# Two DRAM tensors for the experts' rows, and eight index buffers in place of five

## The chip, the cores and the metric

The kernel runs on one core of one Trainium2 chip. The metric is the device time of one execution in microseconds (us). The core has five engines that each run their own list of instructions: PE (matmul), DVE (vector), ACT (scalar), POOL (GpSimd) and SP, which here only issues DMAs. They meet by semaphores.

## The reference

512 tokens of width 1024 pass through two blocks. The first ends in a mixture of experts, and that is where the change lies. Cut to what matters:

```python
scores = sigmoid(h @ router_w)                        # 64 experts
idx = top_8(scores + router_b, in the best 4 of 8 groups of experts)
wts = scores[idx] / sum(scores[idx]) * 2.5
def body(acc, blk):                                   # blocks of up to 128 tokens of one expert
    tok, wt, e = blk
    xb = h[tok]
    hid = silu(xb @ w1[e]) * (xb @ w3[e])             # 1024 -> 256
    return acc.at[tok].add(wt[:, None] * (hid @ w2[e])), None   # 256 -> 1024
routed, _ = scan(body, zeros, blocks)
shared = (silu(h @ sw1) * (h @ sw3)) @ sw2
f = routed + shared
x = layernorm(DN_ALPHA * x + g2 * f, ln2_w, ln2_b)    # DN_ALPHA = 2 ** 0.25
```

The second block (attention and a feed-forward network) follows and is not touched.

## The kernel before, in words

**Lists.** The 64 experts are worked off as 39 token lists of at most 128 tokens: eleven with one expert each (the "singles", numbered 0 to 10), then thirteen of two experts that share one list (the "pairs"), two more singles and thirteen more pairs. The program calls a list b and an expert's job e0, e1, ... by its place in the sequence.

**One list.** `find(b)` makes the list: DVE compares each token's place with a row of numbers (`oh`, L1324), PE multiplies that with the token numbers (`sel`), and DVE writes `idx` (L1329, the token numbers as integers) and `wt` (L1330, the weights). POOL gathers the 128 rows from the DRAM tensor `hrows` by an indirect DMA (`xg`, L1683). PE transposes them (`tsp`, L1149); ACT and DVE split them in two parts, `xh` and `xl` (L122, L123), since each product is made of three matmuls of split factors (L128 to L130). 24 matmuls give `gu`; ACT applies silu, DVE multiplies (`hid`, L1344). PE transposes `hid` (`ht`), it is split (`th`, `tl`), and 12 matmuls give `y`. DVE multiplies `y` by the gate `g2b` into `yo` (L1443, two halves). POOL adds `yo` to the rows of the DRAM tensor `yrows` by an indirect DMA that accumulates (L1687, the scatter).

**Weights.** Each expert has three pieces (g0, g1, o2) of 128x2048 in 32 bits. SP loads them, ACT casts them to a high part (h), DVE subtracts that to get a low part (l, L123, 128x2048).

**What sets the order.** The loop over jobs at the end of `moe` writes the second half of a job (`down` and the scatter) behind the first half of the next one (`late`). `find` runs two lists ahead. The framework's scheduler orders each engine's list by its own estimates, and it puts a wait wherever a buffer is used again: a tile with `bufs=5` is written again five uses later, once its last reader is done. For `idx` the last reader is the scatter's DMA. DMAs on one DRAM tensor that write are ordered one behind the other.

**Beginning and end.** The four 128-token parts of the shared expert run first. POOL adds x (already times DN_ALPHA) to their rows (L1461), and SP writes them into `yrows` (L1462): the start value of the sum. `overflow` (L1629, a loop) would take lists beyond the 39; here it runs no iteration, but at its entry and exit the engines wait for all DMAs. Behind it `combine` loads x from `yrows` (L1607) and normalizes it: DVE's `l2st`, `l2mv`, POOL and DVE's `l2rs`, then x scaled by `ln_w`, `ln_b`.

Of the kernel before, what the change touches and what calls it, by code (L numbers as in the profile page):

```python
# [13 lines left out]
F32 = mybir.dt.float32  # L14
# [3 lines left out]
U32 = mybir.dt.uint32  # L18
AF = mybir.ActivationFunctionType
OP = mybir.AluOpType  # L20
# [4 lines left out]
P = 128  # L25
D = 1024
KT = D // P
T = 512
TC = 256
TA = T + TC  # L30
NT = T // P
# [62 lines left out]
class Kernel:  # L94
# [1273 lines left out]
    def moe(self):  # L1368
# [3 lines left out]
        nc, I = self.nc, self.I  # L1372
        V, G = nc.vector, nc.gpsimd
        E = 64
        self.hrows = self.dram.tile([T, D], F32, name="hrows")
        self.yrows = self.dram.tile([T, D], F32, name="yrows")

        cx = self.mcx = ExitStack()
        sp = self.pool("slots", ctx=cx, side="right")
# [12 lines left out]
        with ExitStack() as c2:  # L1392
            self.grans(self.pool("ew", ctx=c2), 2, 5)
            es = self.pool("es", bufs=2, ctx=c2)
# [4 lines left out]
            def job(name, gr, x, put, wt=None, first=True, last=True):  # L1399

                hid = self.hidden(name, gr, es, *x, wt)
                if late:
                    late.pop()()
                late.append(lambda: sums.append(self.down(name, gr[2], es, hid, put, () if first else sums[-1], first, last)))

            sums, idx, ahead = [], {}, []
# [11 lines left out]
            def find(b):  # L1418

                if b < len(groups):  # L1420
                    idx[b] = [es.tile([P, n], dt, tag=tag, name=f"{tag}{b}", bufs=5) for n, dt, tag in ((1, U32, "idx"), (2, F32, "wt"))]
                    self.select(es, idx[b][0], idx[b][1][:, :share(b)], *groups[b][0], f"sel{b}")

            def begin():
                find(0)
                self.gather(xg[0], idx[0][0])
                find(1)
# [7 lines left out]
            def putter(name, end):  # L1435

                yo = []

                def put(half, py):
                    if half == 0:  # L1440
                        yo.append(es.tile([P, D], F32, tag="yo", name="yo" + name))
                    hs = slice(half * 512, half * 512 + 512)
                    V.tensor_tensor(yo[0][:, hs], py, self.g2b[:, hs], OP.mult)  # L1443
                    if half == 1:
                        end(yo[0])
                return put

            src = lambda w: [w[:, i * 2048:(i + 1) * 2048] for i in range(3)]
            with ExitStack() as c3:
                sh = []  # L1450

                def shared_load(i):
                    sh.append(self.load(src(I["sh_pack"])[i], f"shg{i}"))

                def shared_parts(i):
                    sh[i] = self.parts(sh[i])

                def shared(t):

                    def end(y):  # L1460
                        G.tensor_tensor(y, y, self.x[:, t], OP.add)  # L1461
                        nc.sync.dma_start(self.yrows[t * P:(t + 1) * P, :], y)  # L1462
                    job(f"sh{t}", sh, self.hT[t], putter(f"sh{t}", end))
                shared = {"L": shared_load, "W": shared_parts, "s": shared, "e": first_load, "E": first_parts}
                self.mix_out(c3, shared, begin)
# [7 lines left out]
            gr = old = None  # L1473
            for n, (b, c, h) in enumerate(jobs):
                if n == 1:
                    with ExitStack() as c3:
                        self.order(self.pool("ol", ctx=c3))
                new = n == 0 or jobs[n - 1][1] != c
                if h == 0:
                    find(b + 2)  # L1480
                if new:
                    if c < NX:
                        w = I["exp_pack"][c]
                    else:
                        with self.tc.issue_after(self.loaded):
                            er = nc.values_load(self.ids[:, c - NX:c - NX + 1], engines=(mybir.EngineType.SP,), min_val=0, max_val=63)
                        w = I["exp_pack"][bass.ds(er, 1)].rearrange("e p n -> p (e n)")
                    w = src(w)

                    if c < 2:  # L1490
                        gr, ahead = ahead[:2], ahead[2:]
                        gr = [g if ("E", 2 * c + n) in MIX else self.parts(g) for n, g in enumerate(gr)]
                    else:
                        gr = [self.gran(w[i], f"e{c}g{i}") for i in range(2)]
                if old:
                    old[0].append(self.gran(old[1], f"e{c}o2"))
                old = (gr, w[2]) if new else None
                if h == 0:
                    x = xg[b % 2]
                    if b:  # L1500
                        self.gather(x, idx[b][0])
                    xh = ep.tile([P, KT, P], F32R, tag="xh", name=f"xh{b}")
                    xl = ep.tile([P, KT, P], F32R, tag="xl", name=f"xl{b}")
                    self.transpose_split(xh, xl, [x])
                job(f"e{n}", gr, (xh, xl), putter(f"{b}", lambda y, b=b: self.scatter(y, idx[b][0])),
                    idx[b][1][:, h:h + 1], h == 0, h == share(b) - 1)
                if not new:
                    late.pop()()
# [91 lines left out]
    def combine(self, loaded, done):  # L1600

        nc = self.nc
        V, G = nc.vector, nc.gpsimd
        with self.mcx as cx:
            m2 = self.pool("cmb", bufs=NT, ctx=cx, side="right")
            for t in range(NT):
                nc.sync.dma_start(self.x[:, t], self.yrows[t * P:(t + 1) * P, :])  # L1607
            loaded()
            lw, lb = self.ln2
            for t in range(NT):  # L1610
                x = self.x[:, t]
                if t < 2:
                    self.normalize(m2, x, x, lw, lb, "l2")
                else:
                    mu, rs = self.ln_stats(m2, x, LN_EPS, "l2")
                    V.scalar_tensor_tensor(x, x, mu, lw, OP.subtract, OP.mult)
                    nc.scalar.activation(x, x, AF.Copy, scale=rs)
                    G.tensor_tensor(x, x, lb, OP.add)
                done(t)

    def overflow(self, sp):

        nc, I = self.nc, self.I
        V, G = nc.vector, nc.gpsimd
# [3 lines left out]
        n = nc.values_load(self.ntot, min_val=0, max_val=E)  # L1628
        with self.tc.For_i(0, n):  # L1629
            with ExitStack() as cx:  # L1630
# [19 lines left out]
                gr = [self.gran(w[:, i * 2048:(i + 1) * 2048], f"ovg{i}") for i in range(3)]  # L1650
# [14 lines left out]
                idx = op.tile([P, 1], U32, name="oidx")  # L1665
                wt = op.tile([P, 1], F32, name="owt")
                self.select(op, idx, wt, lambda t: pj[:, t:t + 1], lambda t: tk[:, t:t + 1], "osel")
                x = op.tile([P, D], F32, name="oxg")
                G.memset(x, 0.0)
                self.gather(x, idx)  # L1670
                xh = op.tile([P, KT, P], F32R, name="oxh")
                xl = op.tile([P, KT, P], F32R, name="oxl")
                self.transpose_split(xh, xl, [x])
                yo = op.tile([P, D], F32, name="oyo")
# [2 lines left out]
                    hs = slice(half * 512, half * 512 + 512)  # L1677
                    V.tensor_tensor(yo[:, hs], py, self.g2b[:, hs], OP.mult)
                self.down("ov", gr[2], op, self.hidden("ov", gr, op, xh, xl, wt), put)
                self.scatter(yo, idx)  # L1680

    def gather(self, x, idx):
        self.nc.gpsimd.indirect_dma_start(out=x, out_offset=None, in_=self.hrows, in_offset=bass.IndirectOffsetOnAxis(ap=idx, axis=0),  # L1683
                                          bounds_check=T - 1, oob_is_err=False)

    def scatter(self, y, idx):
        self.nc.gpsimd.indirect_dma_start(out=self.yrows, out_offset=bass.IndirectOffsetOnAxis(ap=idx, axis=0), in_=y, in_offset=None,  # L1687
                                          bounds_check=T - 1, oob_is_err=False, compute_op=OP.add)


# [599 lines left out]
```

## Time and profile before

| | |
|---|---|
| median of 3 runs | 2989.39 us (2989.31 to 2990.99) |
| the profiled execution | 2991.12 us, its span 2989.3 us |
| PE busy | 2672.5 us, 89% of the span |
| DVE busy | 1880.2 us, 63% |
| ACT busy | 1263.1 us, 42% |
| POOL busy | 530.0 us, 18% |

The span is the part of the execution that the profiler sees. Busy shares are means over the whole program. The expert stage runs from about 740 to 1521 us; the singles fill its first third.

### The profile page before, as it was taken

What the parts mean: (1) busy time and instruction counts of PE and PEld (TensorE: products, weight loads), DVE (VectorE), ACT (ScalarE), POOL (GpSimd) and SP (SyncE); (2) the same over time, 40 slices, a digit from 0 to 9 for tenths busy, and PEclk for the clock granted to TensorE, in tenths of its full rate; (3) what the DMA queues carried; (4) which work ended last, traced back from release to release, by engine and by line L of the source; (5) the groups of instructions that cost most, each with busy time, mean ns of one, the idle gap of its engine ahead of it and who ended that gap; (6) DMA issues with size and microseconds to landing.
All of it is one profiled execution on the core that took longest, in us unless ns stands there. A gap on an engine that the chain in (4) does not pass through costs nothing. (4 is left out here: it accounts for less than half of the span.)

```text
span 2989.3 us, 46834 instructions
## 1 busy us (share of the span) xinstructions
PE 2672.5 (89%) x18599; PEld 2261.3 (76%) x18603; DVE 1880.2 (63%) x3463; ACT 1263.1 (42%) x1976; POOL 530.0 (18%) x514
## 2 busy tenths in 40 slices
PE   6999776779776999999959999999998999999998
PEld 4787565668655777777758999887877989987786
DVE  6974767768765899899958943332326974433233
ACT  4232432323343676676735554321225556422221
POOL 1001341121223213222233420000002341000000
PEclk9999777989887999999979999999999999999999
DMA  6541002124576999999932112222222211222222
GB/s 213 198 151 43 5 26 38 31 95 163 205 232 218 327 389 359 329 376 355 342 119 72 57 57 71 85 95 82 92 93 100 69 59 50 86 85 90 94 92 78
DMA packets 134348, 427.52 MB, mean 143 GB/s; under 512 B 51194, under 2 KB 77754, under 8 KB 95728
## 3 DMA queue, kind: packets, MB, share of 16 engines
q1 hardware_dynamic: 122896, 391.77, 36.7%
q0 software_dynamic: 11232, 32.74, 4.5%
q8 instruction: 147, 2.41, 0.3%
q14 instruction: 73, 0.60, 0.1%
HBM read 398.25 MB, written 34.37 MB: 145 GB/s over the span
## 5 line engine op out<-in xcount | busy, mean ns | idle before, releaser
L1687 POOL DMA_INDIRECT yrows<-yo,idx x39 | 109.6, 2810 | 321.3 <-DVE yo L1443 203.1
L2066 DVE TENSOR_TENSOR hd<-hd,ffu 128x512 f32<-128x512 f32 x44 | 30.3, 688 | 178.0 <-PE ffu L130 178.0
L1683 POOL DMA_INDIRECT xg<-hrows,idx x39 | 86.3, 2213 | 214.5 <-PE tsp L1149 135.0
L122 ACT CAST hh<-hd 128x512 fp32r<-128x512 f32 x44 | 27.2, 618 | 109.6 <-DVE hd L2066 109.6
L137 POOL TENSOR_TENSOR nm1s<-nm1s,cst 128x1 f32<-128x1 f32 x4 | 2.2, 550 | 381.6 <-DVE nm1s L136 373.7
L137 POOL TENSOR_TENSOR frss<-frss,cst 128x1 f32<-128x1 f32 x4 | 2.2, 548 | 372.2 <-DVE frss L136 372.2
L2085 DVE TENSOR_TENSOR x<-x,dn 128x512 f32<-128x512 f32 x32 | 22.0, 686 | 66.0 <-PE dn L130 66.0
L871 PE MATMUL qa<-PR,qk 64*64 64x128 f32 (+1 forms) x384 | 27.0, 362 | 33.1 <-DVE PR L977 12.7
L1329 DVE CAST idx<-sel 128x1 uint32<-128x1 f32 x39 | 6.0, 154 | 77.9 <-DMA yrows<-yo,idx 60.5
L1958 ACT COPY pTs<-pT 128x128 f32<-128x128 f32 (+3 forms) x96 | 39.9, 428 | 35.5 <-PE pT L1956 33.4
L2065 ACT ACTIVATE hd<-ffg 128x512 f32<-128x512 f32 x44 | 26.0, 592 | 67.2 <-PE ffg L130 67.0
L1925 DVE MAX8 m<-sc 128x8 f32<-128x256 f32 (+2 forms) x96 | 52.9, 555 | 1.0
L1926 DVE MATCH_REPLACE8 sc<-m,sc 128x256 f32<-128x256 f32 (+2 forms) x96 | 52.0, 542 | 0.0
L123 DVE TENSOR_TENSOR xl<-tsp,xh 128x512 fp32r<-128x512 f32 x78 | 51.0, 682 | 1.4 <-ACT xh L122 1.3
L1149 PE MATMUL tsp<-cst,xg 128*128 128x128 f32 x312 | 45.5, 283 | 6.8 <-DMA xg<-hrows,idx 6.8
L237 DVE SCALAR_TENSOR_TENSOR adas<-adar,cs,adas 128x256 f32<-128x256 f32 x112 | 49.9, 475 | 1.3
L122 ACT CAST xh<-tsp 128x512 fp32r<-128x512 f32 x78 | 42.8, 592 | 18.2 <-PE tsp L1149 18.2
L871 PEld LDWEIGHTS qa<-PR,qk 64*64 64x64 f32 x384 | 19.2, 193 | 37.2 <-issue 14.4
L1960 PE MATMUL po<-va,pTs 128*128 128x64 f32 x320 | 45.0, 275 | 1.0 <-ACT pTs L1958 0.3
L1960 PEld LDWEIGHTS po<-va,pTs 128*128 128x128 f32 x320 | 40.3, 191 | 6.0 <-ACT pTs L1958 5.2
L1149 PEld LDWEIGHTS tsp<-cst,xg 128*128 128x128 f32 x312 | 36.4, 145 | 9.9 <-issue 7.1
L1712 PE MATMUL nm0p<-nm0d,x 128*128 128x128 f32 x64 | 14.1, 414 | 30.3 <-DVE l2rs L136 21.7
(4409 smaller groups left out, 10492.3 us busy)
## 6 DMA issues: line engine op xcount, KB each, us to landing
adar<-in_ada_w_dram SPq DMA_DIRECT2D x16, 1024.0 KB
x<-in_w_in_pack_dram SPq DMA_DIRECT2D x11, 1024.0 KB
adaw<-in_ada_w_dram SPq DMA_DIRECT2D x8, 1024.0 KB
x<-in_x_dram SPq DMA_DIRECT2D x8, 512.0 KB
xs<-x SPq DMA_DIRECT2D x8, 512.0 KB
x<-xs SPq DMA_DIRECT2D x8, 512.0 KB
hrows<-h SPq DMA_DIRECT2D x4, 512.0 KB
yrows<-yosh SPq DMA_DIRECT2D x4, 512.0 KB
```

What stands on the lines that cost most here:

```text
L122: nc.scalar.copy(h, src)
L123: nc.vector.tensor_tensor(l, src, h.bitcast(F32), OP.subtract)
L237: V.scalar_tensor_tensor(acc, wt[:, k], c, acc, OP.mult, OP.add)
L871: nc.tensor.matmul(pq[h][cs, x, m, :nw], qk[hs, x, m, cs], PR[hs, m, :nw, cs], start=True, stop=True)
L1149: nc.tensor.transpose(pt[:, (k - k0) * w + j * P:(k - k0) * w + (j + 1) * P], x[:, k * P:(k + 1) * P], self.ident)
L1683: self.nc.gpsimd.indirect_dma_start(out=x, out_offset=None, in_=self.hrows, in_offset=bass.IndirectOffsetOnAxis(ap=idx, axis=0), bounds_ch ...
L1687: self.nc.gpsimd.indirect_dma_start(out=self.yrows, out_offset=bass.IndirectOffsetOnAxis(ap=idx, axis=0), in_=y, in_offset=None, bounds_ch ...
L1925: V.max(m8, s)
L1926: V.match_replace(s, m8, s, PICKED)
L1958: nc.scalar.copy(st, pt)
L1960: nc.tensor.matmul(out, st[:, s], v[:, s, c0:c0 + w], start=(s == 0), stop=(s == n - 1))
L2066: V.tensor_tensor(hd, hd, ps[1], OP.mult)
```

## The change

The sum is kept in two DRAM tensors, `yrows[0]` and `yrows[1]`. The scatter of list b goes to `yrows[b % 2]` (those of the overflow loop to `yrows[0]`). `yrows[0]` starts from the shared expert's rows, `yrows[1]` from x, which SP writes there; the addition on POOL is gone. `combine` loads both and adds them on DVE. And the tiles `idx` and `wt` get eight buffers in place of five.

```diff
-        self.yrows = self.dram.tile([T, D], F32, name="yrows")
+        self.yrows = [self.dram.tile([T, D], F32, name=f"yrows{i}") for i in range(2)]
...
-                    idx[b] = [es.tile([P, n], dt, tag=tag, name=f"{tag}{b}", bufs=5) for n, dt, tag in ((1, U32, "idx"), (2, F32, "wt"))]
+                    idx[b] = [es.tile([P, n], dt, tag=tag, name=f"{tag}{b}", bufs=8) for n, dt, tag in ((1, U32, "idx"), (2, F32, "wt"))]
...
                 def shared(t):
+                    rows = slice(t * P, (t + 1) * P)
+                    nc.sync.dma_start(self.yrows[1][rows, :], self.x[:, t])
                     def end(y):
-                        G.tensor_tensor(y, y, self.x[:, t], OP.add)
-                        nc.sync.dma_start(self.yrows[t * P:(t + 1) * P, :], y)
+                        nc.sync.dma_start(self.yrows[0][rows, :], y)
...
-                job(f"e{n}", gr, (xh, xl), putter(f"{b}", lambda y, b=b: self.scatter(y, idx[b][0])),
+                job(f"e{n}", gr, (xh, xl), putter(f"{b}", lambda y, b=b: self.scatter(b % 2, y, idx[b][0])),
...
             for t in range(NT):
-                nc.sync.dma_start(self.x[:, t], self.yrows[t * P:(t + 1) * P, :])
+                nc.sync.dma_start(self.x[:, t], self.yrows[1][t * P:(t + 1) * P, :])
+            ys = [m2.tile([P, D], F32, tag="y0", name=f"y0{t}") for t in range(NT)]
+            for t in range(NT):
+                nc.sync.dma_start(ys[t], self.yrows[0][t * P:(t + 1) * P, :])
             loaded()
             lw, lb = self.ln2
             for t in range(NT):
                 x = self.x[:, t]
+                V.tensor_tensor(x, x, ys[t], OP.add)
...
-    def scatter(self, y, idx):
-        self.nc.gpsimd.indirect_dma_start(out=self.yrows, ...
+    def scatter(self, i, y, idx):
+        self.nc.gpsimd.indirect_dma_start(out=self.yrows[i], ...
```

The scheduler orders the engines anew. The rows below are instructions in program order with their waits (PE, DVE, Activation: that engine; DMAHW: a plain DMA, DMASW: one of POOL's indirect DMAs).

DVE before, from yo of list 4 (`yo_9186`) to yo of list 5 (`yo_9307`); `idx_9320` is list 9's and lies in the buffer of list 4's.

```order
L1443 TENSOR_TENSOR yo_9186<-e4y_9179,g2b 128x512 [waits PE_49]
L1443 TENSOR_TENSOR yo_9186<-e4y_9188,g2b 128x512 [waits PE_49]
L123 TENSOR_TENSOR e8g0l<-e8g0r,e8g0h 128x2048 [waits DMAHW3_49,Activation_49]
L123 TENSOR_TENSOR xl_9250<-tsp,xh_9249 128x512 [waits Activation_49] x2
L123 TENSOR_TENSOR e5tl<-e5ht,e5th 128x256 [waits Activation_49]
L123 TENSOR_TENSOR e8g1l<-e8g1r,e8g1h 128x2048 [waits DMAHW4_49,DVE_49]
L1329 CAST idx_9320<-sel_9322 128x1 [waits DMASW5_49,PE_49]
L1330 TENSOR_REDUCE wt_9321<-sel_9322 128x1 [waits DVE_49]
...
L123 TENSOR_TENSOR e8o2l<-e8o2r,e8o2h 128x2048 [waits DMAHW5_49,Activation_49]
L1344 SCALAR_TENSOR_TENSOR e6hid<-e6hid,wt_8958,e6gu 128x256 [waits Activation_49]
L1443 TENSOR_TENSOR yo_9307<-e5y_9300,g2b 128x512 [waits PE_49]
```

DVE in the changed kernel, in the same place: `yo_9187` is list 4's, `yo_9308` list 5's, `idx_9321` list 9's.

```order
L1444 TENSOR_TENSOR yo_9187<-e4y_9180,g2b 128x512 [waits DMASW1_49,PE_49]
L1444 TENSOR_TENSOR yo_9187<-e4y_9189,g2b 128x512 [waits PE_49]
L1329 CAST idx_9200<-sel_9202 128x1 [waits DMASW0_49,PE_49]
...
L123 TENSOR_TENSOR e5tl<-e5ht,e5th 128x256 [waits DVE_49,Activation_49]
...
L123 TENSOR_TENSOR e8g0l<-e8g0r,e8g0h 128x2048 [waits DMAHW7_49]
L123 TENSOR_TENSOR e8g1l<-e8g1r,e8g1h 128x2048 [waits DMAHW0_49,DVE_49]
L1344 SCALAR_TENSOR_TENSOR e6hid<-e6hid,wt_8959,e6gu 128x256 [waits DVE_49,Activation_49]
L1444 TENSOR_TENSOR yo_9308<-e5y_9301,g2b 128x512 [waits DMASW3_49,DVE_49,PE_49]
L123 TENSOR_TENSOR e8o2l<-e8o2r,e8o2h 128x2048 [waits DMAHW1_49,DVE_49]
L1444 TENSOR_TENSOR yo_9308<-e5y_9310,g2b 128x512 [waits PE_49]
L1329 CAST idx_9321<-sel_9323 128x1 [waits DMASW2_49,PE_49]
```

In the first piece the cast of list 9's `idx` waits for DMASW5, the scatter of list 4. In the second the cast's DMASW waits are gathers of earlier lists, yo's first half waits for a scatter two lists back (DMASW1 that of list 2, DMASW3 that of list 3), and the split of o2 stands between yo's halves.

POOL before, scatters of lists 4 to 6 and gathers of lists 9 and 10 (`yo_9186` is list 4's).

```order
L1687 DMA yrows<-yo_9186,idx_8735 512x1024 [waits DMASW3_49,DVE_49]
L1683 DMA xg_8443<-hrows,idx_9320 128x1024 [waits DMASW2_49,DVE_49,PE_49]
L1687 DMA yrows<-yo_9307,idx_8846 512x1024 [waits DMASW5_49,DVE_49]
L1683 DMA xg_7147<-hrows,idx_9441 128x1024 [waits DMASW4_49,DVE_49,PE_49]
L1687 DMA yrows<-yo_9428,idx_8957 512x1024 [waits DMASW7_49,DVE_49]
```

POOL in the changed kernel, the same place; `yrows_7124` and `yrows_7125` are `yrows[0]` and `yrows[1]`, `yo_9187` is list 4's.

```order
L1694 DMA yrows_7124<-yo_9187,idx_8736 512x1024 [waits DMASW1_49,DVE_49]
L1690 DMA xg_7148<-hrows,idx_9200 128x1024 [waits DMASW0_49,DVE_49,PE_49]
L1694 DMA yrows_7125<-yo_9308,idx_8847 512x1024 [waits DMASW3_49,DVE_49]
L1690 DMA xg_8445<-hrows,idx_9321 128x1024 [waits DMASW2_49,DVE_49,PE_49]
L1694 DMA yrows_7124<-yo_9429,idx_8958 512x1024 [waits DMASW4_49,DVE_49]
```

Before, each scatter waits for the scatter of the list ahead of it; now for that of two lists ahead.

SP in the changed kernel, from the last weights to the overflow loop (L1636, whose branches are left out here); before, only `ln_w` and `ln_b` stood between the weights and the loop, and all loads of x behind it.

```order
L1181 DMA eg2r<-in_exp_pack_dram 128x2048 [waits DMAHW4_49,DVE_49]
L1610 DMA x<-yrows_7125 128x1024 [waits DMASW4_49]
L1155 DMA ln_w<-in_ln_w_dram 128x1024 [waits PE_49]
L1155 DMA ln_b<-in_ln_b_dram 128x1024 [waits DMAHW5_49]
L1610 DMA x<-yrows_7125 128x1024 [waits DMAHW6_49]
L1610 DMA x<-yrows_7125 128x1024 [waits DMAHW7_49]
L1610 DMA x<-yrows_7125 128x1024 [waits DMAHW0_49]
```

The four loads of `yrows[1]` have moved ahead of the loop, the first behind the scatter of list 37 (DMASW4); the four loads of `yrows[0]` stand behind the loop.

## Rows read from the trace of the kernel before

**Rows 1.** The page's group of line 1329: busy, mean ns, idle before, releaser.

```profile
L1329 DVE CAST idx<-sel 128x1 uint32<-128x1 f32 x39 | 6.0, 154 | 77.9 <-DMA yrows<-yo,idx 60.5
```

**Rows 2.** Waits, 740 to 980 us: total us, times, longest.

```profile
DVE idx L1329 <- DMA yrows<-yo,idx: 60.5, 8, 9.7
...
POOL xg L1683 <- DMA yrows<-yo,idx: 20.3, 2, 11.9
```

**Rows 3.** Stretches: length, busy us per engine (instructions), clock, DMA share, GB/s.

```profile
740.00:818.00 78.00, 61.12 (x335) 48.21 (x334) 58.72 (x188) 26.77 (x32) 15.24 (x10) 0.85 0.54 194
836.00:983.00 147.00, 100.37 (x434) 74.98 (x434) 86.53 (x124) 57.78 (x56) 48.71 (x17) 0.79 0.69 219
1040.00:1120.00 80.00, 79.49 (x395) 63.76 (x395) 77.01 (x86) 57.78 (x51) 15.11 (x9) 1.00 1.01 389
...
1521.00:1548.00 27.00, 8.60 (x40) 8.12 (x40) 23.18 (x51) 14.37 (x37) 13.02 (x10) 0.56 0.71 263
...
983.00:998.00 15.00, 14.68 (x55) 11.27 (x55) 12.61 (x11) 7.72 (x5) 3.31 (x2) 0.85 0.94 320
```

**Rows 4.** Timeline of POOL: start, length, instruction, idle before it and releaser.

```profile
836.01 3.42 POOL L1687 DMA_INDIRECT yrows<-yo,idx  x1 [4.19 <-DVE yo L1443]
...
869.95 3.38 POOL L1687 DMA_INDIRECT yrows<-yo,idx  x1 [0.97 <-DVE yo L1443]
...
889.55 3.38 POOL L1687 DMA_INDIRECT yrows<-yo,idx  x1 [3.34 <-DVE yo L1443]
...
982.88 3.38 POOL L1687 DMA_INDIRECT yrows<-yo,idx  x1 [0.96 <-DVE yo L1443]
997.95 2.69 POOL L1687 DMA_INDIRECT yrows<-yo,idx  x1 [11.69 <-DMA yrows<-yo,idx]
```

**Rows 5.** Timeline of DVE, same columns, in the singles.

```profile
884.28 0.16 DVE L1329 CAST idx<-sel 128x1 uint32<-128x1 f32 x1 [8.69 <-DMA yrows<-yo,idx]
...
887.99 1.28 DVE L1443 TENSOR_TENSOR yo<-e4y,g2b 128x512 f32<-128x512 f32 x2
889.19 2.28 DVE L123 TENSOR_TENSOR e8g0l<-e8g0r,e8g0h 128x2048 fp32r<-128x2048 f32 x1
...
977.80 0.16 DVE L1329 CAST idx<-sel 128x1 uint32<-128x1 f32 x1 [8.69 <-DMA yrows<-yo,idx]
...
981.32 1.28 DVE L1443 TENSOR_TENSOR yo<-e9y,g2b 128x512 f32<-128x512 f32 x2
...
990.92 2.29 DVE L123 TENSOR_TENSOR e38o2l<-e38o2r,e38o2h 128x2048 fp32r<-128x2048 f32 x1 [2.39 <-ACT e38o2h L122]
...
993.52 1.28 DVE L1443 TENSOR_TENSOR yo<-e10y,g2b 128x512 f32<-128x512 f32 x2
```

**Rows 6.** Operations on yrows, whole span: DMA from issue to landing.

```profile
DMA to landing us min/median/max: 6.1/12.3/15.2
```

**Rows 7.** Timeline of PE, the same columns, behind one of those waits.

```profile
924.57 0.69 PE L1353 MATMUL e7ht<-cst,e7hid 128*128 128x128 f32 x2 [6.41 <-DVE e7hid L1344]
```

**Rows 8.** Timelines of POOL, DVE and PE around the first gather.

```profile
764.97 2.37 POOL L1461 TENSOR_TENSOR yosh<-yosh,x 128x1024 f32<-128x1024 f32 x1 [9.53 <-DVE tok L1311]
764.76 0.16 DVE L1311 CAST tok<-wr 128x4 bf16<-128x4 f32 x1
765.15 2.22 DVE L1311 CAST tok<-wr 128x4 bf16<-128x4 f32 x1
768.08 1.27 POOL L1683 DMA_INDIRECT xg<-hrows,idx  x1 [0.74 <-DVE idx L1329]
778.64 0.88 PE L1149 MATMUL tsp<-cst,xg 128*128 128x128 f32 x3 [6.81 <-DMA xg<-hrows,idx]
```

**Rows 9.** Timelines and chain of waits (start, length, what) around the end.

```profile
1497.20 3.35 POOL L1687 DMA_INDIRECT yrows<-yo,idx  x1 [14.74 <-DVE yo L1443]
1510.26 6.07 DMA yrows<-yo,idx
1517.27 3.79 DMA x<-yrows
1522.72 1.27 DVE L1162 SCALAR_TENSOR_TENSOR x<-x,l2mv,ln_w 128x1024 f32<-128x1024 f32 x1
1527.84 1.52 POOL L137 TENSOR_TENSOR l2rs<-l2rs,cst 128x1 f32<-128x1 f32 x1 [3.41 <-DVE l2rs L136]
1529.34 0.54 POOL L137 TENSOR_TENSOR nm0s<-nm0s,cst 128x1 f32<-128x1 f32 x1
```

More of the change, by code (lines that the diff above doesn't have):

```diff
@@ L1679, in overflow @@
                 self.down("ov", gr[2], op, self.hidden("ov", gr, op, xh, xl, wt), put)
-                self.scatter(yo, idx)
+                self.scatter(0, yo, idx)
     def gather(self, x, idx):
@@ L1684, in gather @@
                                           bounds_check=T - 1, oob_is_err=False)
-    def scatter(self, y, idx):
-        self.nc.gpsimd.indirect_dma_start(out=self.yrows, out_offset=bass.IndirectOffsetOnAxis(ap=idx, axis=0), in_=y, in_offset=None,
+    def scatter(self, i, y, idx):
+        self.nc.gpsimd.indirect_dma_start(out=self.yrows[i], out_offset=bass.IndirectOffsetOnAxis(ap=idx, axis=0), in_=y, in_offset=None,
                                           bounds_check=T - 1, oob_is_err=False, compute_op=OP.add)
```

## The prediction

> **What bounds the kernel now.** I read the page's costliest groups first, then the table of waits of the expert stage, the busy time by stretches, the timelines of POOL and DVE, and last the beginning and the end of the stage. The reader is to see one thing in the first two: DVE's idx cast at L1329 works 6.0 us in the whole span and stands idle 77.9 us before it, 60.5 of them for the landing of a scatter [rows 1]; the table has the same 60.5 us between 740 and 980 us, in 8 waits of up to 9.7 us, so all of them lie there. POOL stood 20.3 us for landings too, but POOL has time [rows 2].
>
> The stretches show where that is. From 836 to 983 us, where the lists of one expert run, no engine is full: PE 100.37 of 147 us at a granted clock of 0.79, DVE 86.53, the DMA engines at a share of 0.69. From 1040 to 1120 us, in the paired lists, PE has 79.49 of 80 us at a clock of 1.00 and DMA a share of 1.01, and nothing there waits for a scatter [rows 3]. So the change can pay in the singles only; the pairs are at PE's and the DMA engines' limit and I leave them as they are (their order of instructions is the same but for single swaps).
>
> Why the cast waits: there are five idx buffers, so the cast of list b+5 overwrites the indices that the scatter of list b still reads. On DVE that cast stands only six instructions behind yo(b), whose scatter has just been issued. The rows show the circle closed: the scatter issued at 869.95 lands, the cast goes at 884.28 after 8.69 us of waiting (14.3 us from issue), yo follows at 887.99, the next scatter at 889.55 [rows 4, 5]. Over eight lists, from the scatter at 836.01 to that at 982.88, one list takes 146.87 / 8 = 18.36 us [rows 4]. A landing takes 6.1 / 12.3 / 15.2 us (shortest, median, longest) [rows 6].
>
> PE's waits are this wait handed on: hid stands behind the cast on DVE, PE's transposes of hid wait 6.41 us for it, and while PE idles its clock falls, hence the 0.79 [rows 3, 7].
>
> **The change, part by part.** *Buffers and tensors.* With eight idx buffers the cast reuses the indices of a scatter eight lists back; that wait goes. The single DRAM tensor alone would keep each scatter behind the landing of the one before: the last single list shows it, where the scatter at 997.95 stood 11.69 us for a landing and came 15.07 us after the one at 982.88 [rows 4]. With two tensors a scatter waits for that of two lists back. Both edits are needed for a step under about 15 us, and both are there.
>
> *What is late next.* After the change yo(b) carries a wait on the landing of scatter(b-2), since there are two yo buffers; it is there now but covered. Scatter follows yo by 889.55 - 887.99 = 1.56 us [rows 4, 5], and in the new order one 2.28 us split stands between yo's halves, so a step T must satisfy 2T >= landing + 1.56 + 2.28. With 15.2 us that is T >= 9.5 us. This wait doesn't bind unless T gets below that or landings lengthen. Behind it on DVE stand the other half of yo, the next idx and the splits, so it would cost in full if it bound.
>
> *The step without waits.* Below: DVE's own work, (146.87 - 60.46) / 8 = 10.80 us, where 60.46 are the eight waits [rows 2, 4]. PE's work is 100.37 / 8 = 12.55 us at the mixed clock, times 0.79 some 9.9 us at the full one. The DMA engines need 0.69 x 18.36 = 12.7 us at the present share, or, as 219 GB/s x 18.36 us = 4.02 MB per list, 10.3 us at the pairs' 389 GB/s [rows 3]. One row pair shows a step as it will be: behind the last of the eight waits, yo of list 9 goes at 981.32 and yo of list 10 at 993.52 with no scatter's landing between them, 12.20 us; DMA moves 320 GB/s at a share of 0.94 beside it [rows 3, 5]. I take 12.2 us, between 10.8 and 12.7. That is 8 x (18.36 - 12.2) = 49.3 us off; by the ends 60.5 and 45.3. Of the 60.46 us of waits so about 11 come back, as waits for PE, ACT and weights that the landing covers now.
>
> *The beginning.* The four adds on POOL (L1461) go. One hurts now: it starts at 764.97 and runs 2.37 us; beside it DVE's small tok cast takes 2.22 us where such a cast takes 0.16; behind that come idx, the first gather at 768.08 and PE's 6.81 us wait for it [rows 8]. Worth 2.06 us. In return SP issues four writes of x, 0.5 MB each, ahead of the stores of hrows. Moved at this stretch's rate for busy engines, 194 / 0.54 = 359 GB/s [rows 3], 2.1 MB are 5.8 us, which lie in DMA engines idle for half of the stretch, and the gather comes late enough to cover them. Bounds: -6.8 (PE's whole wait goes) to +5.8 (the writes shown in full); I take -2.1.
>
> *The end.* DVE gets four adds of 128x1024. The nearest rows are its 1.27 us operations of that size [rows 9]; all four, 5.1 us. The first stands alone on the path. The others fall into a stretch where DVE is busy 23.18 of 27 us [rows 3], so about half of them shows. The loads of yrows[1] stand on SP before the overflow loop, behind the landing of list 37's scatter: issued 1497.20, by the median at 1509.5, by the longest landing at 1512.4. Four loads at 263 / 0.71 = 370 GB/s are 5.7 us, and ln_w and ln_b, which stand behind the first of them, 2.8 us more: done between 1515 and 1521, while the last scatter lands at 1516.33 and the loads of before began at 1517.27 [rows 9]. So hidden, or up to 3.7 us late. The four loads of yrows[0] behind the loop stand where the loads of x stood and cost no more. Bounds: 1.3 to 5.1 + 3.7 = 8.8; I take +3.
>
> A row speaks for the upper part: POOL's 128x1 step of rstd takes 1.52 us at 1527.84, beside DVE's 1.27 us operation, and 0.54 us at 1529.34 [rows 9]. The Trainium skill, "SBUF — State Buffer" (Who interferes with whom), has a rule for that: a DVE instruction with two SBUF inputs contends with a GpSimd instruction that reads SBUF, and whoever issues first holds the pair for the whole instruction. By the rule each new add holds up whatever POOL has then, and the end costs 5.1 rather than 3.
>
> *The sum.* -49.3 - 2.1 + 3 = -48.4 us. The profiled execution took 2991.12 us; 2991.12 - 48.4 = 2942.7. It stood 1.73 us over the median of 2989.39, from which the forecast is 2941 us.
>
> **The rivals.** *A: the landing still counts for half.* If scatters run at the 15.07 us of the one list that waited only for the landing of the scatter before [rows 4], because more traffic stretches gather and scatter, the gain is 8 x (18.36 - 15.07) = 26.3: 2989.4 - 26.3 + 1 = 2964. For it: DMA is at a share of 0.94 in the step that I took as the model. Against it: the pairs move 389 GB/s, and landings are no longer there (15.2 is the longest of all).
>
> *B: DVE's floor.* PE's clock stays up once its idle time per list falls from over 5 us to about 2, and DVE runs without a gap: T = 10.8, 2989.4 - 60.5 + 0.9 = 2930. For it: the pairs, DVE at 77.01 of 80 us and clock 1.00 [rows 3]. Against it: in the model step ACT's split made DVE wait, and the chain from the gathered rows over xh, xl, gu and silu has no second list in hand. The Trainium skill, "TensorE: Matmul & The Clock Gate" (Part 1), says the default state is throttled and activity releases it; by that rule PE would need 9.9 us and DVE alone would bound the step. The row with 0.79 beside the 6.41 us gap agrees with the first half; that the gaps which remain are harmless no row shows.
>
> *C: two scatters in flight slow each other.* Up to now none of the singles' scatters runs while another is in flight; with two tensors they may. The new wait of yo on scatter(b-2) then takes the place of the old one: T = (landing + 3.84) / 2. It ends on the other side where that exceeds 18.36, at a landing over 32.9 us; at 36 us, T = 19.9, 8 x 1.56 = 12.5 us lost, with the ends 2989.4 + 12.5 + 0.9 = 3003. Against it: gathers and weights run beside scatters now, and landings stay under 15.2 even at full DMA load.
>
> *D: the wait only changes its name,* with landings near 32 us or with another buffer that I overlooked: about 2990.
>
> **How the numbers follow.** Forecast (T from 11.5 to 13): 0.70, 2941, with its own range from T and the two ends 2930 to 2954. B 0.12, A 0.12, D 0.03, C 0.03. The range that leaves out a fifth at most goes from 2926 (B with a better beginning) to 2964 (A). A change of 0.2%, 6 us, is what a measurement of this kernel can tell from none: faster 0.94 (forecast, A, B), same 0.03 (D), slower 0.03 (C).
>
> **What would show it.** In the profile after, idx L1329 has no wait for a scatter's landing; scatters in the singles come every 12.2 us; PE's clock from the second list on is over 0.9, DMA over 300 GB/s; the pairs keep 18.5 to 20.2 us. At the beginning no DVE cast of 2 us stands before the first idx. At the end DVE's first l2st comes 1 to 4 us later after the last scatter's landing than now. I am wrong if yo L1444 shows waits for a scatter, if landings pass 20 us, or if the step falls under 11 or stays over 13.5.

## The result, and the profile after

| | before | changed |
|---|---|---|
| median | 2990.19 us (2989.31 to 2997.06, 4 runs) | 2927.22 us (2924.79 to 2929.51, 4 runs) |
| ratio of the times | | 0.9779, 95% interval 0.9759 to 0.9799 |
| span of the profiled execution | 2989.3 us | 2927.7 us |

The kernel is faster by 2.2%, 66 us by the ratio and 61.6 us between the two spans. 48.4 us were forecast, 2941 us. The median lies 1.2 us above the lower end of the range, and the kernel before's median times the ratio, 2924 us, lies 2 us below it. The direction and the main mechanism were right; the gain is larger by 27 to 37%. One of the six executions of e2, below, took 3734.72 us at a granted clock of 0.65; its median here is that of the other five.

Where it came from is read off the same marks in both traces: the last store of hrows, the starts of the scatters on POOL, the landing of the last one, and the load of the next stage's third weights (`wi0kb0r` on SP). Differences of those starts, in us:

| from - to | before | after | difference | forecast |
|---|---|---|---|---|
| last store of hrows - scatter 0 | 70.1 | 66.3 | -3.8 | -2.1 |
| scatter 0 - 1 | 17.7 | 12.4 | -5.3 | 0 |
| scatter 1 - 9 | 146.9 | 91.7 | -55.2 | -49.3 |
| scatter 9 - 11 | 29.9 | 28.0 | -1.9 | 0 |
| scatter 11 - 38 | 497.5 | 492.6 | -4.9 | 0 |
| scatter 38 - landing | 6.1 | 7.9 | +1.8 | (end: +3) |
| landing - next stage's third weights | 57.3 | 64.2 | +6.9 | |

The sum is -62.4; what lies outside gives 0.8 back. The last mark, before and then after:

```profile
1573.66 0.33 SPq L1181 DMA_DIRECT2D wi0kb0r<-in_w_in_pack_dram  x1
```

```profile
1512.11 0.33 SPq L1181 DMA_DIRECT2D wi0kb0r<-in_w_in_pack_dram  x1
```

The singles first: POOL's timeline (start, length, instruction, idle before and releaser), which answers to [rows 4].

```profile
827.79 2.99 POOL L1694 DMA_INDIRECT yrows<-yo,idx  x1 [0.31 <-issue]
...
874.04 1.58 POOL L1694 DMA_INDIRECT yrows<-yo,idx  x1 [8.23 <-DVE wt L1330]
...
885.34 1.58 POOL L1694 DMA_INDIRECT yrows<-yo,idx  x1 [8.31 <-DVE wt L1330]
...
896.64 1.58 POOL L1694 DMA_INDIRECT yrows<-yo,idx  x1 [8.30 <-DVE wt L1330]
...
919.45 1.58 POOL L1694 DMA_INDIRECT yrows<-yo,idx  x1 [8.53 <-DVE wt L1330]
```

From the second to the tenth scatter one list takes 91.66 / 8 = 11.46 us, and 11.3 where the rhythm is settled. No scatter waits for a landing. DVE shows the same step; the columns are those of [rows 5].

```profile
881.57 0.69 DVE L1444 TENSOR_TENSOR yo<-e6y,g2b 128x512 f32<-128x512 f32 x1 [0.24 <-PE e6y L130]
882.18 2.28 DVE L123 TENSOR_TENSOR e9o2l<-e9o2r,e9o2h 128x2048 fp32r<-128x2048 f32 x1
884.38 0.69 DVE L1444 TENSOR_TENSOR yo<-e6y,g2b 128x512 f32<-128x512 f32 x1
884.98 0.15 DVE L1329 CAST idx<-sel 128x1 uint32<-128x1 f32 x1
885.04 0.15 DVE L1330 TENSOR_REDUCE wt<-sel 128x1 f32<-128x3 f32 x1
885.40 1.29 DVE L123 TENSOR_TENSOR xl<-tsp,xh 128x512 fp32r<-128x512 f32 x2 [0.20 <-ACT xh L122]
```

The idx cast, which waited 8.69 us in the row of before, follows at once, and yo waits a quarter of a microsecond for PE, not for a scatter. The stretches (columns as in [rows 3]: beginning, singles, end, and last the pairs):

```profile
740.00:818.00 78.00, 63.77 (x356) 50.33 (x356) 54.51 (x192) 29.08 (x35) 8.33 (x7) 0.85 0.59 215
828.00:919.00 91.00, 81.64 (x431) 64.74 (x431) 84.11 (x111) 57.69 (x57) 22.74 (x15) 0.98 0.99 341
1451.00:1478.00 27.00, 7.06 (x29) 6.48 (x30) 21.70 (x46) 10.96 (x27) 9.10 (x6) 0.56 0.56 212
...
960.00:1040.00 80.00, 79.11 (x398) 64.38 (x397) 77.42 (x85) 57.78 (x51) 14.77 (x8) 1.00 1.01 390
```

In the singles PE's granted clock rose from 0.79 to 0.98, nearly all at the level of 2.4 GHz, and PE's busy time fell from 100.37 us in 147 to 81.64 in 91, with as many instructions (434 and 431). In the pairs clock, DMA share and GB/s stand as before.

Scatters also land sooner there than they did: the time from issue to landing, first in the singles after, then in those of before.

```profile
DMA to landing us min/median/max: 10.2/10.3/13.0
```

```profile
DMA to landing us min/median/max: 10.1/13.6/15.2
```

And their POOL instruction is shorter, 1.58 us against 3.38. Before, it started inside DVE's 2.28 us split of 128x2048, both inputs of which are in SBUF (889.55 beside 889.19 [rows 4, 5]); now it starts beside idx, wt and the split of xl, which takes one input from PSUM. The Trainium skill, "SBUF — State Buffer" (Who interferes with whom), has a DVE instruction with two SBUF inputs contend with a GpSimd instruction that reads SBUF; these rows agree, with 1.8 us on POOL, if the scatter, whose indices lie in SBUF, counts as such. Where the Trainium skill infers in the same section that a `tensor_tensor` does not stall the descriptor generation of a DMA, these rows differ, and the measurement decides.

The beginning is as forecast: the cast beside POOL's add, 2.22 us, is back at 0.17 and the first gather goes at 766.67 (768.08 before) [rows 8].

```profile
765.32 0.17 DVE L1311 CAST tok<-wr 128x4 bf16<-128x4 f32 x1
```

The end is longer than forecast. The chain of waits (start, length, what), which answers to [rows 9]:

```profile
1440.05 7.87 DMA yrows<-yo,idx
...
1448.85 3.63 DMA y<-yrows
1452.51 1.24 DVE x L1618
1453.77 1.29 DVE l2st L145 x2
1455.05 1.12 DVE x L1618
1456.18 0.12 DVE l2mv L146
1456.30 1.09 DVE x L1618
```

The last scatter takes 1.8 us longer to land; three additions, not one, stand ahead of tile 0's normalization; and tile 0 is done (first store `xs<-x`) 12.5 us after the landing where it was 9.5. 3.8 us more go behind that. There tile 3's statistics come late: its addition is the last on DVE, and between the two halves of its `l2st`, and ahead of its `l2mv`, DVE works and waits for the next stage (`nm0`). Its store comes 38.4 us after the landing (1486.30 on SP), 29.0 before (1545.34).

```profile
1468.12 0.68 DVE L145 BATCH_NORM_STATS2 l2st<-x 128x6 f32<-128x512 f32 x1
...
1472.49 0.29 DVE L1715 TENSOR_SCALAR nm0d<-cst,nm0s 128x128 f32<-128x128 f32 x1 [2.32 <-POOL nm0s L137]
1472.69 0.69 DVE L145 BATCH_NORM_STATS2 l2st<-x 128x6 f32<-128x512 f32 x1
...
1477.25 0.20 DVE L146 BATCH_NORM_AGGREGATE l2mv<-l2st 128x2 f32<-128x12 f32 x1
```

### The profile page after: what moved, and what is told of

It reads as the page before. It is cut to its first block, busy times and chain, and to the rows that moved or that the text cites. A ratio compares the mean times of both kernels' runs of the same rounds, so it can differ in the third digit from the quotient of the medians.

```text
span 2927.7 us, 46888 instructions
## 1 busy us (share of the span) xinstructions
PE 2648.7 (90%) x18599; PEld 2253.6 (77%) x18603; DVE 1876.5 (64%) x3467; ACT 1263.8 (43%) x1976; POOL 491.2 (17%) x510
## 4 chain that ended last, share of the span: by engine, by line
PE 38%; DVE 6%; POOL 3%; ACT 2%; issue 2%; DMA 0%; POOLq 0%; ACTq 0%; SPq 0%; DVEq 0%
PE ffu L128 3%; PE ffu L129 3%; PE ffu L130 3%; PE ffg L130 3%; PE ffg L129 3%; PE ffg L128 3%; PE dn L129 3%; PE dn L130 2%; PE dn L128 2%; PE po L1967 2%; DVE sc L1933 1%; PE wo L129 1%; PE wo L130 1%; PE pT L1963 1%; PE wo L128 1%
## 5 line engine op out<-in xcount | busy, mean ns | idle before, releaser
L1694 POOL DMA_INDIRECT yrows<-yo,idx x39 | 94.8, 2432 | 352.0 <-DVE yo L1444 178.6
L1690 POOL DMA_INDIRECT xg<-hrows,idx x39 | 73.5, 1886 | 173.2 <-PE tsp L1149 122.8
L871 PE MATMUL qa<-PR,qk 64*64 64x128 f32 (+1 forms) x384 | 27.9, 376 | 32.0 <-DVE PR L977 12.6
L1719 PEld LDWEIGHTS nm0p<-nm0d,x 128*128 128x128 f32 x64 | 13.8, 325 | 40.9 <-DVE l2rs L136 28.3
```

What stands on the lines that cost most here:

```text
L1694: self.nc.gpsimd.indirect_dma_start(out=self.yrows[i], out_offset=bass.IndirectOffsetOnAxis(ap=idx, axis=0), in_=y, in_offset=None, bounds ...
```

## The experiments

**One part of the change at a time.** The first two separate its two halves: the changed kernel with five buffers, and the kernel before with eight.

```diff
 e1: -... name=f"{tag}{b}", bufs=8)      in the changed kernel
     +... name=f"{tag}{b}", bufs=5)
 e2: -... name=f"{tag}{b}", bufs=5)      in the kernel before
     +... name=f"{tag}{b}", bufs=8)
```

> The changed kernel with five idx buffers again. If the wait of idx on its own buffer is the whole cause (theory): idx L1329 waits for the landing of the scatter five lists back as in the kernel before, about 60 us in 8 waits, the singles' step is 17.5 to 18.5 us, and what is left is the beginning (-3) and the end (+8.7): about 2995 us, 2988 to 3000. Rival (the one DRAM tensor held the scatters back, the buffers only look guilty): step under 15 us, under 2965 us.

Measured: 2993.81 us, ratio 1.002 (1.0007 to 1.0034). The waits between 740 and 980 us (total, times, longest):

```profile
DVE idx L1329 <- DMA yrows<-yo,idx: 66.7, 9, 9.3
```

Scatters 1 to 9 take 146.25 us, 18.3 a list. Two tensors alone remove nothing: the buffers are the cause of the wait.

> The kernel before with eight idx buffers and nothing else: one DRAM tensor, POOL's adds at the beginning, no adds at the end. By the prediction's reasoning both edits are needed: each scatter waits for the landing of the one before, the step is about 15 us, 2990 - 8 x 3.3 - 4 = 2960 us (2952 to 2966). Rival: in the trace after, the singles' scatters land in 10.3 us (median; 13.6 before), under the step of 11.3 us, so the order behind one another costs nothing: step 11.3 to 11.6, no cost at the end, 2915 to 2925 us, at least as fast as the changed kernel.

Measured: 2924.75 us, ratio 0.9793 (0.9776 to 0.9811). The step is 100.90 / 8 = 12.6 us, not 15, and nearer to the rival. The single tensor does make scatters wait, on POOL:

```profile
POOL yrows L1687 <- DMA yrows<-yo,idx: 34.9, 5, 8.6
```

The median landing is 10.7 us there, so the scatters still follow one another closely:

```profile
867.50 1.57 POOL L1687 DMA_INDIRECT yrows<-yo,idx  x1 [10.37 <-DVE e6hid L1344]
...
879.54 1.58 POOL L1687 DMA_INDIRECT yrows<-yo,idx  x1 [8.61 <-DMA yrows<-yo,idx]
...
890.40 1.80 POOL L1687 DMA_INDIRECT yrows<-yo,idx  x1 [7.61 <-DMA yrows<-yo,idx]
```

What two tensors win in the singles, 9.2 us, is mostly taken back behind them: scatters 9 to 17 take 135.9 us with one tensor and 141.7 with two. From scatter 1 to 17 it is 236.8 against 233.4, 3.4 us for the second tensor; its end costs 72.1 against 62.7 us from the last scatter to the next stage. So eight buffers alone give what the whole change gives, as far as the two ratios tell (0.9793 and 0.9779, each within 0.002).

**The beginning and the end by themselves.** e3 takes the additions on POOL out of the kernel before; e4 takes yrows[1]'s loads and the additions on DVE out of the changed kernel.

```diff
 e3: -                        G.tensor_tensor(y, y, self.x[:, t], OP.add)
 e4: -                nc.sync.dma_start(self.x[:, t], self.yrows[1][t * P:(t + 1) * P, :])
     +                nc.sync.dma_start(self.x[:, t], self.yrows[0][t * P:(t + 1) * P, :])
     -                V.tensor_tensor(x, x, ys[t], OP.add)
```

> The kernel before without the four additions of x on POOL (L1461); it leaves x out of the sum. Measures the beginning alone. Theory: DVE's 2.2 us tok cast, the idx and the first gather come 1.5 to 3 us earlier, and all behind it too: 2986 to 2988 us, every scatter from list 0 on 2 to 3 us earlier. Rival: the gain at the beginning is lost again in the singles, whose step is set by landings: under 0.5 us, 2990.

Measured: 2983.31 us, ratio 0.9983 (0.9972 to 0.9994); from the last store of hrows to scatter 0 64.6 us, 5.5 less than before. In the other profiles without the adds this stretch is 64.2 to 68.6 us (e1 to e9 and the changed kernel); with them 70.1 (before) and 68.8 (e2). The adds cost some 2 to 5 us; my 2.1 is the lower end. Scatters 1 to 9 take 143.8 us in this profile, 3.1 less than before, which the theory does not explain, and the time lies below its range.

> The changed kernel without the loads of yrows[1] and the four additions at the end (combine takes yrows[0] alone, so half of the lists and x are left out). Measures the end alone. Theory: all of the 8.7 us that the trace after loses between the last scatter and the next stage comes back: last scatter lands in about 6 us (7.87 now), no three adds ahead of the first normalization, tile 3's statistics in time: 2917 to 2921 us where the changed kernel takes 2927. Rival (the loss is the next stage's own order, not the adds): under 4 us back.

Measured: 2919.46 us, ratio 0.9773 (0.9758 to 0.9788). The last scatter lands in 6.10 us, and the next stage's third weights come 56.0 us behind that: by these marks all of the 8.7 us, and 1.3 more, belong to the additions and what goes with them (tile 3 is stored 28.7 us after the landing). The times alone would not show it: the ratio's interval overlaps the changed kernel's.

**Ways to a cheaper end.** e6 frees yrows[1] one list earlier; e7 and e9 add the tensors up in DRAM while lists still run; e11 moves half of the additions to POOL. e5 is the changed kernel again, on one chip with e6, e7 and e8; e9 to e14 have no changed kernel on theirs.

```diff
 e6:  +self.scatter(b % 2 if b < 37 else 0, y, idx[b][0])
 e7:  +self.scatter(b % 2 if b < 36 else 0, y, idx[b][0])
      +if b == 36 and h == 0:
      +    G.dma_start(self.yrows[0], self.yrows[1], accum_op=OP.add, max_dma_last_dim=4096)
 e9:  35 in place of 36 in both
 e11: e6, and in combine
      +(V if t < 2 else G).tensor_tensor(x, x, ys[t], OP.add)
```

> The changed kernel unaltered, beside the next three on one chip, so that their few us can be told from the differences between chips: ratio to before 0.977 to 0.980, 2921 to 2929 us, singles' step 11.3 us, last scatter landing in 7 to 8 us.

Measured: 2928.02 us, ratio 0.9802 (0.9779 to 0.9826).

> The changed kernel, but list 37's scatter goes to yrows[0], so that yrows[1] is complete one list earlier and its loads and those of ln_w and ln_b go out before the last scatter. If they slowed the last scatter's landing (theory: 7.87 us after against 6.07 before, DMA share 0.89 against 0.46 beside it): landing back at 6 to 6.3 us, end 1.5 to 2 us shorter, the rest of the end as in the changed kernel. Rival (the landing is slow for another reason): 7.5 us and no difference.

Measured: 2929.51 us, ratio 0.9807 (0.9784 to 0.9831). The chain shows the landing back where it was:

```profile
1430.98 6.03 DMA yrows<-yo,idx
```

The loads of x, ln_w and ln_b beside it had slowed it. The rest of the end is no shorter than in the changed kernel (65.3 us, 64.2 there), and the median shows no gain.

> The changed kernel, with the two tensors added up by one accumulating DMA in DRAM behind list 35's scatter; lists 36 to 38 then go to yrows[0], and combine is the kernel before's (no adds on DVE, four loads). If the 8.7 us at the end come from the adds and the traffic that go with them (theory), they come back: 0.997 of the changed kernel, 6 to 9 us less, 2916 to 2921 us, last scatter landing in 6 us. Rival: 2 MB added up in DRAM take over 20 us and hold the scatter of list 36, yo of list 38 and the weights: the last lists come 5 to 15 us later, and nothing is gained.

Measured: 2922.64 us, ratio 0.9788 (0.9764 to 0.9811), 5 us under e5 on the same chip, with intervals that overlap. The end is 63.4 us, the kernel before's, but the rival is half right too: the merge is slow, and the last three scatters queue behind it.

```profile
1400.87 22.82 DMA yrows<-yrows
1424.45 6.26 DMA yrows<-yo,idx
1431.44 6.32 DMA yrows<-yo,idx
1438.50 6.12 DMA yrows<-yo,idx
```

> As the kernel with the accumulating DMA, one list earlier: behind list 34's scatter; lists 35 to 38 go to yrows[0]. There the DMA took 22.8 us and moved the last scatter 3.8 us back. If its lateness was that cost (theory): from first to last scatter 624 to 625 us as in the changed kernel, end 63 us, 2912 to 2918 us. Rival: it now runs beside weights at full DMA load and slows them: the lists come later by more than is saved, 2919 to 2925 us.

Measured: 2922.92 us, ratio 0.9783 (0.9761 to 0.9806). The time is the rival's. First to last scatter take 630.3 us, 5.6 over the changed kernel, in a profile of the slowest of the five executions (2932.06 us). Whether the merge slowed the weights or only held up the scatters behind it, this run doesn't tell apart.

> The changed kernel with list 37's scatter to yrows[0] and tiles 2 and 3 added up on POOL rather than DVE. Tells whether the end is long for DVE's additions and their order or for POOL's. If DVE's order is it (theory: two adds ahead of tile 0's statistics, and the second half of tile 3's behind the next stage's work): from the landing to the load of the next stage's third weights 59 to 61 us (64.2 after, 57.3 before). Rival: POOL's adds and DVE's work hold each other up: 63 us or more.

Measured: 2925.59 us, ratio 0.9796 (0.9771 to 0.982). From the last scatter to the next stage's third weights 72.6 us pass, 72.1 in the changed kernel: the rival. POOL's additions and DVE's normalization stretch each other, DVE's 1.27 us operation to 3.31.

```profile
1449.00 3.27 POOL L1618 TENSOR_TENSOR x<-x,y 128x1024 f32<-128x1024 f32 x1 [11.51 <-DVE l2st L145]
```

```profile
1450.76 2.58 DVE L1162 SCALAR_TENSOR_TENSOR x<-x,l2mv,ln_w 128x1024 f32<-128x1024 f32 x1
...
1453.87 3.31 DVE L1163 SCALAR_TENSOR_TENSOR x<-x,l2rs,ln_b 128x1024 f32<-128x1024 f32 x1
```

**What sets 11.3 us.** Four kernels put work on, or take it off, in the singles.

```diff
 e8:  o2 of experts 3 to 10: DVE makes l for 1024 of 2048 columns, POOL zeroes the rest
 e12: lists 4 to 10, each: +nc.sync.dma_start(extra, w[0][:, :1024])      # DRAM to DRAM
 e13: g1 of experts 3 to 10: ACT casts 1024 of 2048 columns, POOL zeroes the rest
 e14: o2 of experts 3 to 10: 1024 of 2048 columns are loaded, POOL zeroes the rest
```

> The changed kernel with 1.1 us less of DVE's work per single list: the low parts of o2 are made for half of the columns in experts 3 to 10, the other half is set to zero by POOL (leaves out part of the weights' low bits). Tells what bounds the step of 11.3 us. If DVE does (85 of 92 us busy in the trace after; theory): 10.2 to 10.6 us, seven steps, 5 to 8 us less in all. Rival (the DMA engines, at a share of 0.99 and 342 GB/s, or PE with its xh): still 11.2 to 11.4.

Measured: 2925.71 us, ratio 0.9792 (0.9763 to 0.9821); the settled steps are 11.26 to 11.28 us. DVE doesn't set the step.

> The changed kernel with 0.5 MB more to copy per single list (lists 4 to 10, DRAM to DRAM, read and written). Tells whether the DMA engines set the step of 11.3 us. If they do (share 0.99, 342 GB/s, and 0.5 MB at that rate are 1.5 us): 12.6 to 13.5 us in lists 4 to 9, 7 to 12 us more up to list 17. Rival (PE, ACT and the chain over xh set it, DMA only keeps up): 11.3 to 11.6 us, under 3 us more.

Measured: 2941.49 us, ratio 0.9843 (0.9815 to 0.987); scatters 1 to 9 take 101.0 us, 9.4 more. But it is uneven: three steps grow (to 18.75, 12.63 and 15.88 us), others stay at 11.2 to 11.5. Up to scatter 17 it is 8.9 us more, as the theory has it, but not as a longer step in every list. Neither theory is cleanly met: there is no spare room for weights, and yet it isn't they that set a settled step.

> The changed kernel with 0.5 MB less to load per single list: half of o2's columns in experts 3 to 10 are not loaded but set to zero by POOL (leaves out half of these experts' outputs). If the circle over ACT and PE sets the step (theory): still 11.2 to 11.4 us. Rival (DMA's supply): 9.9 to 10.5 us, and up to list 17 some 8 to 10 us less.

Measured: 2924.62 us, ratio 0.9782 (0.9758 to 0.9806); the steps behind scatter 6 are 11.30, 11.29 and 11.52 us, but by then the last of the halved loads is through (355 GB/s). The two steps that test it are those from scatter 4 to 6, first here and then in the changed kernel:

```profile
858.33:880.83 22.50, 20.17 (x110) 15.89 (x110) 21.52 (x30) 14.41 (x15) 6.22 (x5) 1.00 1.01 321
```

```profile
862.87:885.34 22.47, 20.14 (x110) 15.82 (x110) 21.53 (x30) 14.34 (x15) 5.32 (x4) 1.00 1.02 361
```

With 321 in place of 361 GB/s the two steps take as long, though the DMA engines' share stays at 1.01.

> The changed kernel with ACT's cast of g1 made for half of the columns in experts 3 to 10 (0.9 us less between silu and xh), the other half of the high part is zero (leaves out part of these weights' splitting). If the circle silu, casts of g0 and g1, xh, 24 matmuls, silu sets the step (theory): 10.3 to 10.6 us in the steps where it holds. Rival (DMA's supply sets it): still 11.2 to 11.4.

Measured: 2924.52 us, ratio 0.9789 (0.9762 to 0.9816); scatters 4 to 7 come 10.78, 10.95, 10.81 and 10.50 us behind the one before (10.29, 11.17, 11.30 and 11.30 in the changed kernel), and 11.5 again in the two lists behind. Three of the steps fall, by 0.2 to 0.8 us, less than the 0.9 cut from ACT, since the next limit stands close: over the four steps from scatter 3 to 7, 10.76 us each, DVE is busy 42.67 of 43.04 us.

```profile
849.66:892.70 43.04, 41.18 (x220) 31.14 (x220) 42.67 (x61) 24.92 (x29) 20.15 (x12) 1.00 1.01 348
```

Scatters 1 to 9 take 85.9 us, 5.8 less, but 5.0 of it is the one step from scatter 1 to 2 (10.29 us for 15.29); 3.8 of the gain goes again between scatters 9 and 11, where ACT waits for weights. ACT's timeline of the changed kernel shows the circle that was cut:

```profile
880.44 0.38 ACT L1340 ACTIVATE e7hid<-e7gu 128x256 f32<-128x256 f32 x1 [0.76 <-PE e7gu L130]
880.72 1.90 ACT L122 CAST e10g0h<-e10g0r 128x2048 fp32r<-128x2048 f32 x1
882.97 1.91 ACT L122 CAST e10g1h<-e10g1r 128x2048 fp32r<-128x2048 f32 x1 [0.35 <-ACT e10g0h L122]
884.79 1.06 ACT L122 CAST xh<-tsp 128x512 fp32r<-128x512 f32 x2
...
891.73 0.38 ACT L1340 ACTIVATE e8hid<-e8gu 128x256 f32<-128x256 f32 x1 [0.76 <-PE e8gu L130]
```

PE's first matmul of the next list waits for xh:

```profile
885.42 0.50 PE L128 MATMUL e8gu<-e9g0h,xh 128*128 128x512 f32 x1 [1.18 <-ACT xh L122]
```

silu at 880.44, the casts of g0 and g1 and xh behind it, PE from 885.42 on, silu again at 891.73: 11.29 us, of which ACT has 5 and PE 6.3. In the settled steps none of the five engines is full, and though the DMA engines' share is 1.02, the table of waits has none for a load of weights; the circle has no slack.

```profile
862.87:919.45 56.58, 50.64 (x276) 39.87 (x277) 54.36 (x76) 36.24 (x36) 13.38 (x10) 1.00 1.02 359
```

**A version with one tensor and no additions on POOL.** One tensor, eight buffers, and the shared expert's rows added to x by accumulating DMAs in place of POOL's additions (e10, and on one chip with the changed kernel e16 and e15).

```diff
 in the kernel before, with bufs=8:
+                    nc.sync.dma_start(self.yrows[rows, :], self.x[:, t])
                     def end(y):
-                        G.tensor_tensor(y, y, self.x[:, t], OP.add)
-                        nc.sync.dma_start(self.yrows[t * P:(t + 1) * P, :], y)
+                        G.dma_start(self.yrows[rows, :], y, accum_op=OP.add, max_dma_last_dim=4096)
```

> One tensor, eight idx buffers, the start value made by x's write and four accumulating DMAs of the shared expert's rows in place of POOL's adds; combine as before. If the second tensor buys nothing in the sum and the adds on POOL cost 3 to 5 us (theory): 66 us or less from the last store of hrows to the first scatter (69 to 70 with the adds), then 628 and 62.7 as in the kernel with one tensor and eight buffers: 2913 to 2921 us. Rival: the accumulating DMAs collide with the first gathers and the first scatter waits for them: 68 us or more, 2920 to 2926 us.

Measured: 2919.29 us, ratio 0.9784 (0.9756 to 0.9812); hrows to scatter 0 67.1 us, between the theory's 66 and the rival's 68, then 627.7 and 62.4. The time is in the theory's range.

> The changed kernel, for comparison with the next one on the same chip: 0.978 to 0.980 of the kernel before.

Measured: 2923.67 us, ratio 0.9789 (0.9766 to 0.9812).

> One tensor, eight idx buffers, the shared expert's rows added by accumulating DMAs. If the second tensor costs more at the end (9 us) than it gives between first and last scatter (3 us; theory): 4 to 8 us less than the changed kernel on the same chip. Rival (the two are equal and the segments of single profiles mislead): within 2 us.

Measured: 2919.07 us, ratio 0.9774 (0.9749 to 0.9798). The median is 4.6 us less than the changed kernel's. The two intervals overlap, but four of the five executions here are shorter than every one of e15's, whose shortest is 2921.63 us; by the marks it is 6.3 us (from the last store of hrows to the next stage's third weights 757.0 against 763.3), 2.5 lost between the scatters and 9.2 won at the end. With e2 it was not compared on one chip.

## Why the prediction missed

*The wait and its cure* were right: idx on its own buffer (e1), gone in the profile after; PE's clock up with it.

*The step of 12.2 us failed first.* I took it from yo at 981.32 to yo at 993.52 [rows 5], as "a step as it will be". It was not: it began with PE just out of a wait, and a part of its matmuls ran at the 1.2 GHz level; its stretch has a clock of 0.85, and PE is busy 14.68 of its 15.00 us [rows 3], so that PE at that clock is likely what set it. The row of PE in the kernel before:

```profile
981.46 0.69 PE L1353 MATMUL e10ht<-cst,e10hid 128*128 128x128 f32 x2 [6.90 <-DVE e10hid L1344]
```

Settled, the step is the circle's 11.3 us (e8, e13, e14); 11.46 on average, 5.9 us more gain than forecast. Rival B had the clock right and the engine wrong: DVE's floor of 10.8 is there, e13 runs into it, but the circle stands above it.

*The eight lists were too few*, and that is the larger part, 12.1 us that the sum put at nothing. I counted the steps that held a wait put down to a landing. List 1 (-5.3) held a ninth. In the kernel before the profile puts it down to PE, but the cast starts just as scatter 0 lands (818.36 + 10.1 us); in e1 the same cast's wait is put down to the landing. Before, then e1:

```profile
828.54 0.16 DVE L1329 CAST idx<-sel 128x1 uint32<-128x1 f32 x1 [6.59 <-PE e1y L130]
```

```profile
827.18 0.16 DVE L1329 CAST idx<-sel 128x1 uint32<-128x1 f32 x1 [6.79 <-DMA yrows<-yo,idx]
```

Lists 10 and 11 took 10.04 and 17.99 us in place of 15.07 and 14.86 (-1.9); what sets them isn't shown. The pairs, which I left as they were because PE and the DMA engines looked full, gained 4.9 us over 27 lists (the second half's period fell from 20.22 to 19.9 us). The last comes with the eight buffers (497.4 in e1, 489.6 in e2 between scatters 11 and 38), not with the tensors. By which of the reordered instructions I did not find out.

*Both edits needed* was wrong. The 15.07 us step with its wait of 11.69 us [rows 4] was that of a scatter that DVE's split delayed on POOL; with eight buffers landings take 10.3 us (10.7 with one tensor), and one tensor suffices for 12.6 us (e2).

*The beginning* was forecast at -2.1 and is -3.8 by the marks, -2 to -5 by e3 and the others.

*The end* was forecast at +3 and is +8.7. The landing's 1.8 us (e6) I had only as loads that come late. They came early: list 37's scatter lands in 7.7 us in both traces, not in the 12.3 that I took, and the loads then slowed the last scatter beside them. That DVE's list would put three additions ahead of the first normalization the new order showed, and I read it as half hidden. The other 3.8 us, with tile 3's late statistics, I had not seen; that they go with the additions the marks of e4 and e7 show, why the scheduler orders it so stays open.

Of the rivals, A, C and D did not come true: at 341 GB/s landings did not grow (10.3 us in the median, 13.0 at most). What C says of two scatters in flight was hardly tried: in the settled steps one has landed, at 10.3 us, before the next goes at 11.3.

The two misses of one sign, the step and the lists (-18.0 with the pairs), and the beginning's -1.7 outweighed the end's +5.7 and left the sum 14 us short. That the time comes as near to the range's lower end as it does is partly luck: without the end's miss, of the other sign, it would lie 5.7 us further off.

## What to carry to other kernels

A buffer that a DMA reads is busy until that DMA has landed, not until it is issued: count an index tile's buffers by landings over steps, and look whether the wait stands ahead of other engines' work. A step taken as a model must come from a stretch in which the engines run as they will later, at the same clock above all; better, follow the circle of dependences and add up its lengths. And when a change has two halves, price each alone: here the cheap half, one number, had nearly all of the gain, and the other paid for itself in the middle only to lose it at the end.

## What the runs showed of the hardware

An indirect scatter of 128 rows of 4 KB took 1.58 or 3.38 us on POOL, by what DVE did beside it, and landed in 10.3 or 13.6 us (medians of the singles). An accumulating DMA of 2 MB from DRAM to DRAM took 22.8 us, with four loads of 0.5 to 1 MB issued beside it. The last scatter lands in 5.7 to 6.2 us alone and in 7.7 to 8.8 beside 3 MB of loads.
